# Three inner norms by split products with constant tiles and one root function, in a one-core decoder step

## The chip, the cores and the metric

The kernel runs on one core of one Trainium2 chip. Its time is that of one execution on the device, in microseconds (us). The core has five engines that work side by side, each through its own queue in order: TensorE (PE in the profile, its weight loads PEld), VectorE (DVE), ScalarE (ACT), GpSimd (POOL) and SyncE (SP), which here only issues transfers. GpSimd and ScalarE can issue transfers too. An instruction that has to wait for another engine holds up everything behind it in its own queue.

## The reference

One inference step of one decoder layer for 256 prompt positions and 8 x 4 sample positions, 288 columns in all, at a model width of 2048:

```python
h = rmsnorm(x, norm1_g)
proj = h @ w_in + b_in                      # 2048 -> 3 x 1024: a, gate, z
u = a * sigmoid(gate)
c = silu(layernorm(depthwise_causal_conv(u, 31 taps), ln_g, ln_b))
p = (multiscale_pool(z) grouped @ pool_w) * pool_scale
x = x + concat(c, p) @ w_out                # 2048 -> 2048
h2 = rmsnorm(x, norm2_g)
x = x + square(relu(h2 @ w_ff1)) @ w_ff2    # 2048 -> 8192 -> 2048
y = rmsnorm(x, norm_f)
```

All inputs are float32. So there are four norms: the first before `w_in`, the layer norm of the conv channels in the middle, the one before the MLP, and the last. The first three are called the inner norms here.

## The kernel before

Activations are kept transposed, channels on the 128 partitions and the 288 columns on the free axis. All large products are made in fp32r from split operands: a float32 tile is cast to fp32r (its high part), the rest is subtracted (its low part), and a product is the sum of three: high by high, low weight by high input, high weight by low input. Weights arrive in blocks of 128x1024 (`wr`), ScalarE casts them (`whi`, L274), and the low part (`wlo`) is made by VectorE (way "V", L279), by GpSimd in two halves (way "G", L282), or by a ScalarE copy of -high (L276) and a transfer issued by GpSimd that adds the block once more from memory (way "D", L277). `WAYS` says which block goes which way; the seven "D" blocks lie in the input projection.

The weights pass in a fixed order: input projection (conv pairs c0 to c7 and pool groups p0 to p3 by `SEQUENCE`), `w_out` of the pool half, `w_out` of the conv half, the MLP. TensorE's order is that of the code: `mm` (L302) chains its products by `issue_after` while `chain` is set, and `between` of `gemm` puts a norm's products at a given place among them. The other engines' order is set by a scheduler, from priorities (`later(by)` lowers them, a negative value raises them) and an estimate of readiness; buffers of the pools decide when a block can follow.

The norms are never applied to an input before its product. The product of the unnormed input is made, and the result is multiplied by a row of 1/root, copied over all partitions:

- first norm: `squares` adds up the squares of x on VectorE and ScalarE, `rsqrt_sums` (L238) sums over partitions with a ones column on TensorE (float32, 96 columns by 1, three times), makes the root and three refinement steps on 96x3 numbers on VectorE, and `spread` (L259) turns that into a row `rb` on 128 partitions with three products by the identity and a ScalarE copy. `conv_pair` multiplies gate and value by `rb`, makes u, and GpSimd makes the sample positions' tap products (`prd`, L464), VectorE the prompt's taps (L461).
- middle norm: `ln_mean` makes the mean with two float32 products by `ones`, `ln_sums` subtracts it, squares and sums, then `rsqrt_sums` and, 24 products later, `spread`. `mixc` (L592 to L598) multiplies, applies silu and splits: the tiles `mx`, inputs of the second half of `w_out`.
- third norm (`second_rows`, L638): split sums times the constant tile `means`, root by ScalarE, `inverse_root` (L231) on full rows of 288.
- last norm: sums of 96x3, `inverse_root`, spreading, multiplication and the way out.

At the start nine float32 products of `ones` keep TensorE busy (L214) while the first weights and inputs come in. `first_split` (L359) prepares the first blocks: ScalarE casts, VectorE scales the first input tile (L367), and subtracts (L373, L376).

## Time and profile before

| | |
|---|---|
| runs, us | 1084.41, 1084.62, 1085.51; median 1084.62 |
| profiled execution, us | 1084.57 |
| its span, us | 1082.8 |
| TensorE busy in the span | 99% |
| VectorE, ScalarE, GpSimd | 59%, 44%, 16% |
| GpSimd busy between 40.5 and 55.3 us | 14.74 of 14.80 us |
| memory traffic, GB/s: first three 40ths of the span, mean | 325, 281, 273; 176 |
| transfers issued by GpSimd | 7, of 512 KB, 5.8 to 9.8 us from issue to landing |

The page's share of busy time is an average over stages. Rows of a timeline read: start (us from the span's start), duration in us, engine, line, operation, written tile <- read tiles, shapes, count of instructions merged into the row, and in brackets how long the engine was idle before and what ended that. Buffer numbers are left out. A float32 product shows as two rows' worth of passes, so nine warm products are x18. In a row of a stretch of time (`40.50:55.30 ...`) stand its length, then busy time and count of PE, PEld, DVE, ACT and POOL, then the granted clock (filled with 1.00 where the trace has no record), the share of the transfer engines and GB/s.

### The profile page before, as it was taken

To read this page: it belongs to the slowest core of one execution; us is meant where nothing else is said; L and a number is where in the kernel's file an instruction comes from. 1 tells how busy PE (TensorE), PEld (TensorE's weight loads), DVE (VectorE), ACT (ScalarE), POOL (GpSimd) and SP (SyncE) were. 2 spreads that over 40 slices of the span, in tenths; PEclk is the share of its full clock that TensorE was granted. 3 is DMA by queue.
4 is the path that set the end of the run, shared out by engine and by line. 5 is a ranking of instruction groups with operands and counts; after the bars stand their busy time and mean duration, and the time that the engine had idled before them with its cause. 6 is when DMAs were issued, how large, how long until landed. Compare 5 with 4: busy or idle time off the path is not lost.

```text
span 1082.8 us, 19572 instructions
## 1 busy us (share of the span) xinstructions
PE 1071.5 (99%) x8198; PEld 1069.9 (99%) x8198; DVE 635.4 (59%) x818; ACT 479.0 (44%) x585; POOL 173.6 (16%) x180
## 2 busy tenths in 40 slices
PE   9999999999999999999999999999999999999996
PEld 9999999999999999999999999999999999999996
DVE  8899999678655544445544444545544445554553
ACT  8654445475544433334443333444433334444441
POOL 0878979512000000000000000000000000000001
PEclk9999999999999999999999999999999999999998
DMA  9896468545555555555555555555555555555522
GB/s 325 281 273 185 137 196 239 176 152 177 173 164 170 172 166 169 174 164 169 171 168 168 175 165 169 174 167 167 174 165 168 174 169 165 173 166 168 173 78 88
DMA packets 58296, 190.71 MB, mean 176 GB/s; under 512 B 6240, under 2 KB 11232, under 8 KB 58208
## 3 DMA queue, kind: packets, MB, share of 16 engines
q1 hardware_dynamic: 56336, 184.35, 53.9%
q0 software_dynamic: 1008, 3.67, 1.9%
q8 instruction: 64, 1.05, 0.4%
q10 hardware_dynamic: 864, 1.44, 0.4%
q14 instruction: 24, 0.20, 0.1%
HBM read 185.16 MB, written 4.28 MB: 175 GB/s over the span
## 4 chain that ended last, share of the span: by engine, by line
PE 77%; issue 20%; ACT 1%; DVE 0%; DMA 0%; POOL 0%; POOLq 0%
PE ac L305 77%; PE pp L305 1%; DMA wr<-in_w 0%; ACT whi L274 0%; POOL xT L720 0%; ACT n L595 0%; DVE wlo L279 0%; PE pt L305 0%; PE pmean L305 0%; POOLq L770 0%; DVE xT L695 0%; DVE n L592 0%; ACT whi L364 0%; ACT mx L597 0%; DVE hx L367 0%
## 5 line engine op out<-in xcount | busy, mean ns | idle before, releaser
L274 ACT CAST whi<-wr 128x1024 fp32r<-128x1024 f32 (+1 forms) x332 | 348.0, 1049 | 551.4 <-PE ac L305 533.5
L279 DVE TENSOR_TENSOR wlo<-wr,whi 128x1024 fp32r<-128x1024 f32 x288 | 353.1, 1226 | 348.5 <-ACT whi L274 348.5
L305 PE MATMUL ac<-ax,whi 128*128 128x288 f32 x2048 | 351.0, 292 | 0.0
L305 PE MATMUL ac<-fx,whi 128*128 128x288 f32 x2048 | 350.2, 292 | 0.0
L305 PEld LDWEIGHTS ac<-ax,whi 128*128 128x128 f32 x2048 | 296.0, 187 | 0.0
L305 PEld LDWEIGHTS ac<-fx,whi 128*128 128x128 f32 x2048 | 295.6, 187 | 0.0
L305 PE MATMUL ac<-ax,wlo 128*128 128x288 f32 x1024 | 217.4, 292 | 0.0
L305 PE MATMUL ac<-fx,wlo 128*128 128x288 f32 x1024 | 216.4, 292 | 0.0
L305 PEld LDWEIGHTS ac<-ax,wlo 128*128 128x128 f32 x1024 | 162.6, 187 | 0.0
L305 PEld LDWEIGHTS ac<-fx,wlo 128*128 128x128 f32 x1024 | 162.3, 187 | 0.0
L305 PE MATMUL ac<-hx,whi 128*128 128x288 f32 x768 | 131.8, 295 | 1.2 <-DVE hx L367 1.2
L720 POOL TENSOR_TENSOR xT<-xT,rf 128x288 f32<-128x288 f32 x4 | 3.1, 795 | 800.1 <-ACT rf L724 800.1
L305 PEld LDWEIGHTS ac<-hx,whi 128*128 128x128 f32 x768 | 112.1, 190 | 1.4 <-ACT hx L369 1.4
L282 POOL TENSOR_TENSOR wlo<-wr,whi 128x512 fp32r<-128x512 f32 x74 | 100.3, 1410 | 35.3 <-ACT whi L274 34.3
L461 DVE SCALAR_TENSOR_TENSOR pc<-u_all,vec,pc 128x256 f32<-128x256 f32 x232 | 99.5, 483 | 1.9 <-ACT pc L458 0.7
L305 PE MATMUL ac<-hx,wlo 128*128 128x288 f32 x384 | 80.1, 294 | 0.0
L305 PEld LDWEIGHTS ac<-hx,wlo 128*128 128x128 f32 x384 | 61.1, 190 | 0.0
L305 PE MATMUL ac<-dx,whi 128*128 128x288 f32 x256 | 46.0, 296 | 0.0
L305 PE MATMUL ac<-mx,whi 128*128 128x288 f32 x256 | 45.1, 294 | 0.1
L664 DVE SCALAR_TENSOR_TENSOR t<-ac,r 128x576 f32<-128x576 f32 x32 | 24.2, 758 | 25.1 <-PE ac L305 25.1
L305 PEld LDWEIGHTS ac<-dx,whi 128*128 128x128 f32 x256 | 38.0, 188 | 0.2
L305 PEld LDWEIGHTS ac<-mx,whi 128*128 128x128 f32 x256 | 37.5, 188 | 0.6 <-ACT mx L597 0.4
(133 smaller groups left out, 533.6 us busy)
## 6 DMA issues: line engine op xcount, KB each, us to landing
wr<-in_w SPq DMA_DIRECT2D x335, 512.0 KB, 3.8
wlo<-in_w POOLq DMA_DIRECT2D x7, 512.0 KB, 7.7
xT<-in_xT SPq DMA_DIRECT2D x8, 288.0 KB, 7.3
wr<-in_w SPq DMA_DIRECT2D x5, 256.0 KB, 3.6
out_u_out<-u_all SPq DMA_DIRECT2D x1, 1208.0 KB, 9.3
u_all<-in_hist_c SPq DMA_DIRECT2D x8, 136.0 KB, 6.2
out_z_out<-z_all SPq DMA_DIRECT2D x1, 668.0 KB, 9.9
z_all<-in_hist_p SPq DMA_DIRECT2D x4, 152.0 KB, 7.5
```

Source lines behind the costliest of these rows:

```text
L274: nc.scalar.copy(hi, raw)
L279: nc.vector.tensor_tensor(lo, raw, f32(hi), op=ALU.subtract)
L282: nc.gpsimd.tensor_tensor(lo[:, j : j + 2, :], raw[:, j : j + 2, :], f32(hi[:, j : j + 2, :]), op=ALU.subtract)
L305: last = nc.tensor.matmul(*args, **kw)
L461: nc.vector.scalar_tensor_tensor(out=dst, in0=up[:, w : w + SEQ], scalar=cwv[:, w : w + 1], in1=pc, op0=ALU.mult, op1=ALU.add)
L664: nc.vector.scalar_tensor_tensor(out=t, in0=bk[:, :, :T], scalar=0.0, in1=both(rows2[0]), op0=ALU.max, op1=ALU.mult)
L720: eng.tensor_tensor(xk, xk, r[:, None, :].to_broadcast([P, n, T]), op=ALU.mult)
```

## The change

- Warm products: 13 in place of 9. The first scaled input tile is issued ahead of VectorE's first subtractions. The table loaded at the start, before the middle norm and before the third is that of `Abs_reciprocal_sqrt` instead of `Sqrt`.
- `inverse_root` now makes the 1/root in one ScalarE function with epsilon as its bias, and three refinement steps on VectorE; the reciprocal is gone. `rsqrt_sums` and `spread` are gone.
- First norm: the summed squares are split (cast on ScalarE, subtraction on VectorE), two fp32r products by `means` give the mean on all partitions, and `inverse_root` works on full rows of 288. All of it stands at one place of TensorE's queue, inside the third pair's products.
- Middle norm: the two summands of the mean are split (one on GpSimd, one on VectorE), four fp32r products by a new constant tile `means_c`; the sums are split, two products, `inverse_root` on full rows, at one place 60 products before the first one of `mx`.
- VectorE's additions and subtractions of the middle norm are written as `scalar_tensor_tensor`, the form of the taps. Several pieces get a raised priority.

```diff
-    for j in range(9):
+    for j in range(13):
         nc.tensor.matmul(warm[:, 0, 0:P], ones, ones, start=True, stop=True)
...
+    means_c = const.tile([P, P], F32R, name="means_c")
+    nc.gpsimd.tensor_scalar(means_c, ones, 1.0, None, op0=ALU.mult)
...
-    def inverse_root(mean, root, y, out):
+    def inverse_root(mean, y, t, out, after=None):
-        nc.vector.reciprocal(y, root)
-        nc.vector.scalar_tensor_tensor(out=root, in0=mean, scalar=EPS, in1=y, op0=ALU.add, op1=ALU.mult)
...
+        nc.scalar.activation(y, mean, AF.Abs_reciprocal_sqrt, bias=eps[: y.shape[0], :])
         if after is not None:
+            load_table(after, y[:, 0:1])
+        nc.vector.scalar_tensor_tensor(out=t, in0=mean, scalar=EPS, in1=y, op0=ALU.add, op1=ALU.mult)
+        nc.vector.scalar_tensor_tensor(out=t, in0=t, scalar=-0.5, in1=y, op0=ALU.mult, op1=ALU.mult)
+        nc.vector.scalar_tensor_tensor(out=out, in0=t, scalar=1.5, in1=y, op0=ALU.add, op1=ALU.mult)
...
             if k == 0:
-                nc.vector.tensor_scalar(hx[k][0], xT[:, k, :], v("norm1_g", k), None, op0=ALU.mult)
+                first = nc.vector.tensor_scalar(hx[k][0], xT[:, k, :], v("norm1_g", k), None, op0=ALU.mult)
...
         for b in blocks:
-            nc.vector.tensor_tensor(lo[:, b], raw[:, b], f32(hi[:, b]), op=ALU.subtract)
+            with tc.issue_after(first.ins) if k0 == 0 else nullcontext():
+                nc.vector.tensor_tensor(lo[:, b], raw[:, b], f32(hi[:, b]), op=ALU.subtract)
...
-        return [tot[0][:, 0, :]]
+        hs1 = actp.tile([P, 4, T], F32R, name="hs1", tag="p", bufs=4)
+        split_sums = [hs1[:, k, :] for k in range(2)]
+        nc.scalar.copy(split_sums[1], tot[0][:, 0, :])
+        nc.vector.scalar_tensor_tensor(out=split_sums[0], in0=tot[0][:, 0, :], scalar=1.0, in1=f32(split_sums[1]), op0=ALU.mult, op1=ALU.subtract)
+        return split_sums
...
     def first_sums():
-        diag.append(rsqrt_sums(squares(), 1.0 / D, AF.Sigmoid))
-        return diag[0][2]
-
-    def first_rows():
-        pr, last = spread(diag[0])
-        nc.scalar.copy(rb, pr)
+        with later(-LATER):
+            bk = ms("pt")
+            mean, root = bk[:, 0, :T], bk[:, 1, :T]
+            for j, part in enumerate(squares()[::-1]):
+                last = mm(mean, means, part, start=j == 0, stop=j == 1)
+            inverse_root(mean, tmp("y"), root, rb, after=AF.Sigmoid)
         return last
...
-    third = conv_products(2, between={2: first_rows}, classes="01" * 9 + TURN)
+    third = conv_products(2, between={2: first_sums}, classes="01" * 9 + TURN)
...
     def ln_mean():
         norm["mean"] = ms("pmean")[:, 0, :T]
-        mm(norm["mean"], ones, sum_c[:, 0, :], start=True, stop=False)
-        return mm(norm["mean"], ones, cs[-1][:, 1, :], start=False, stop=True)
+        return products(norm["mean"], [hm[:, j, :] for j in (1, 0, 3, 2)])
...
+            hs = actp.tile([P, 4, T], F32R, name="hs", tag="act")
+            low_part(nc.vector, hs[:, 0, :], ssc[:, 0, :], hs[:, 1, :])
+            bk, rl = ms("pt"), row("rl")
+            last = products(bk[:, 0, :T], [hs[:, 1, :], hs[:, 0, :]])
+            norm["rows"] = bk[:, 1, :T]
+            inverse_root(bk[:, 0, :T], rl, norm["rows"], norm["rows"], after=AF.Silu)
         return last
...
-    BETWEEN = {5: {4: ln_mean}, 6: {6: ln_sums}, 7: {2: ln_rows}}
+    BETWEEN = {5: {4: ln_mean}, 6: {6: ln_sums}}
```

Where instructions stand now is shown for three places. GpSimd around its first two "D" transfers (`prd` are the tap products of the sample positions, `wlo` the low parts), before:

```order
L282 TENSOR_TENSOR wlo_608<-wr_603,whi_607 128x512 x2
L464 TENSOR_TENSOR prd_671<-u_all,vec 128x32x31
L464 TENSOR_TENSOR prd_712<-u_all,vec 128x32x31
L277 DMA wlo_613<-in_w 128x1024
L282 TENSOR_TENSOR wlo_622<-wr_617,whi_621 128x512 x2
L282 TENSOR_TENSOR wlo_627<-wr_619,whi_626 128x512 x2
L282 TENSOR_TENSOR wlo_862<-wr_857,whi_861 128x512 x2
L464 TENSOR_TENSOR prd_755<-u_all,vec 128x32x31
L277 DMA wlo_867<-in_w 128x1024
```

And after:

```order
L258 TENSOR_TENSOR wlo_610<-wr_605,whi_609 128x512 x2
L253 DMA wlo_615<-in_w 128x1024
L258 TENSOR_TENSOR wlo_624<-wr_619,whi_623 128x512 x2
L445 TENSOR_TENSOR prd_673<-u_all,vec 128x32x31
L445 TENSOR_TENSOR prd_714<-u_all,vec 128x32x31
L258 TENSOR_TENSOR wlo_629<-wr_621,whi_628 128x512 x2
L258 TENSOR_TENSOR wlo_864<-wr_859,whi_863 128x512 x2
L445 TENSOR_TENSOR prd_757<-u_all,vec 128x32x31
L253 DMA wlo_869<-in_w 128x1024
```

The first transfer and one pair of subtractions have moved ahead of the two tap products; the second transfer has the same work in front of it as before.

VectorE around the middle norm's sums (`q` the squares, `st` and `pt` the roots, `hs` the split sums), before:

```order
L571 TENSOR_TENSOR q_2690<-q_2690 128x288
L279 TENSOR_TENSOR wlo_2805<-wr_2798,whi_2804 128x1024
L249 TENSOR_SCALAR st_2709<-pt_2705 96x3
L253 RECIPROCAL st_2709<-st_2709 96x3
L254 TENSOR_TENSOR st_2709<-st_2709 96x3
L255 SCALAR_TENSOR_TENSOR st_2709<-st_2709 96x3
L256 SCALAR_TENSOR_TENSOR st_2709<-st_2709 96x3
```

And after:

```order
L569 SCALAR_TENSOR_TENSOR q_2699<-q_2699 128x288
L255 TENSOR_TENSOR wlo_2811<-wr_2804,whi_2810 128x1024
L540 SCALAR_TENSOR_TENSOR hs<-q_2699,hs 128x288
L238 SCALAR_TENSOR_TENSOR pt_2717<-pt_2717,rl_2718 128x288
L239 SCALAR_TENSOR_TENSOR pt_2717<-pt_2717,rl_2718 128x288
```

The low half of the sums stands behind the subtraction of a weight block that stood behind TensorE's sums before.

ScalarE from the middle norm's sums to the first normed channels (`n` the silu steps, `mx` their high parts), before:

```order
L274 CAST whi_2804<-wr_2798 128x1024
L250 ACTIVATE st_2709<-st_2709 96x3
L209 ACT_TABLE_LOAD
L209 ACTIVATE few<-st_2709 96x1
L274 CAST whi_2891<-wr_2887 128x1024
L595 ACTIVATE n_2809<-n_2809,vec 128x288 x2
L274 CAST whi_2895<-wr_2889 128x1024
L595 ACTIVATE n_2816<-n_2816,vec 128x288 x2
L597 CAST mx_2813<-n_2809 128x576
```

And after:

```order
L250 CAST whi_2810<-wr_2804 128x1024
L538 CAST hs<-q_2699 128x288
L235 ACTIVATE rl_2718<-pt_2717,cst 128x288
L209 ACT_TABLE_LOAD
L209 ACTIVATE few<-rl_2718,ones 128x1
L250 CAST whi_2897<-wr_2893 128x1024
L250 CAST whi_2901<-wr_2895 128x1024
L595 ACTIVATE n_2815<-n_2815,vec 128x288 x2
L595 ACTIVATE n_2822<-n_2822,vec 128x288 x2
L597 CAST mx_2819<-n_2815 128x576
```

The cast of the high half stands behind a cast of weights, and two casts of weights instead of one now stand ahead of the first silu steps.

More of the change, by code (lines that the diff above doesn't have):

```diff
@@ L572, in ln_sums @@
-        norm["sums"] = rsqrt_sums([ssc[:, 0, :]], 1.0 / DC, AF.Silu)
-        return norm["sums"][2]
-    def ln_rows():
-        norm["rows"], last = spread(norm["sums"])
+        with later(-LATER):
+            ssc = None
+            for c in cs:
+                nc.vector.tensor_tensor(c, c, norm["mean"][:, None, :].to_broadcast([P, 2, T]), op=ALU.subtract)
+                q = tmpp.tile([P, 2, T], F32, name=nm("q2"), tag="ag" if ssc is None else "ag2", bufs=2)
+                nc.scalar.activation(q, c, AF.Square)
+                if ssc is None:
+                    ssc = q
+                else:
+                    nc.vector.scalar_tensor_tensor(out=ssc, in0=ssc, scalar=1.0, in1=q, op0=ALU.mult, op1=ALU.add)
+            nc.vector.scalar_tensor_tensor(out=ssc[:, 0, :], in0=ssc[:, 0, :], scalar=1.0, in1=ssc[:, 1, :], op0=ALU.mult, op1=ALU.add)
+            hs = actp.tile([P, 4, T], F32R, name="hs", tag="act")
[4 more added lines that the diff above has]
+            inverse_root(bk[:, 0, :T], rl, norm["rows"], norm["rows"], after=AF.Silu)
@@ L647, in second_rows @@
         last = mm(mean, means, lo, start=False, stop=True)
-        nc.scalar.activation(root, mean, AF.Sqrt, bias=eps)
-        inverse_root(mean, root, r2, r2)
+        inverse_root(mean, r2, root, r2)
         rows2.append(r2)
```

75 lines of the change are left out of this document (27 added, 48 removed).

## The prediction

> **What bounds the kernel now.** First the engine table and the waits of TensorE, then the chain that ended last, then the timeline at three places. The table and the list of TensorE's waits:
>
> ```profile
> PE 1071.5 (99%) x8198; PEld 1069.9 (99%) x8198; DVE 635.4 (59%) x818; ACT 479.0 (44%) x585; POOL 173.6 (16%) x180
> ...
> PE ac L305 <- DVE hx L367: 1.2, 1, 1.2
> PE ends L712 <- DVE cst L236: 0.2, 1, 0.2
> ```
>
> TensorE is busy 99% of the span. Between warm-up and end it waits once for long, 1.2 us at the very start, and 0.2 us in the last norm. So a step counts only if it takes work off TensorE's own queue, makes its products run faster, or makes TensorE wait where it did not. Durations below are of the profiled execution (1084.57 us: span 1082.8 and 1.8 around it), which agrees with the median of the runs, 1084.62.
>
> Its products, and what the norms add among them, in the chain that ended last:
>
> ```profile
> 32.63 0.43 PE pt L305 x6
> ...
> 35.81 0.84 PE pt L305 x6
> 36.65 73.54 PE ac L305 x564
> ...
> 201.31 0.97 PE pmean L305 x4
> ```
>
> A product of 128x288 costs 73.54/564 = 0.130 us of the stream. The first norm puts 0.43 (sums) and 0.84 (spreading) into it, the middle one 0.97 for its mean and again 0.43 + 0.84.
>
> **Removed products.** First norm: 1.27 becomes two products, 0.26: -1.0 us. Middle norm: 0.97 + 1.27 = 2.24 becomes four and two products, 0.78: -1.46 us. Both would be gains if nothing waited in their place.
>
> **The start.** The warm-up, VectorE's first steps and the first products:
>
> ```profile
> 1.04 4.21 PE L214 MATMUL warm<-ones 128*128 128x128 f32 x18 [1.04 <-DVE cst L229]
> 5.28 0.69 DVE L373 TENSOR_TENSOR wlo<-wr,whi 128x512 fp32r<-128x512 f32 x1 [2.88 <-ACT whi L364]
> 5.89 0.36 DVE L367 TENSOR_SCALAR hx<-xT,vec 128x288 fp32r<-128x288 f32 x1
> 6.40 1.30 PE L305 MATMUL ac<-hx,whi 128*128 128x288 f32 x4 [1.15 <-DVE hx L367]
> ...
> 8.45 2.12 PE L305 MATMUL ac<-hx,whi 128*128 128x288 f32 x8
> ...
> 10.37 0.79 PE L305 MATMUL ac<-hx,wlo 128*128 128x288 f32 x4
> 11.00 1.76 PE L305 MATMUL ac<-hx,whi 128*128 128x288 f32 x12
> ```
>
> The nine warm products (18 passes) end 1.15 us before the first real one, and the 16 real products from 6.40 to 10.37 take 3.97/16 = 0.248 us each, twice the later pace: the clock came up only near 10.4. Thirteen are 26 passes, 26 x 4.21/18 = 6.1 us, until about 7.1: the gap closes. If the clock is up by then, 16 products save 16 x (0.248 - 0.130) = 1.9 us, less up to 0.5 us by which slow warm passes hold the first product back. If it comes up no sooner than before, only those 0.5 us are lost. The scaled input is issued ahead of the subtraction, which frees at most the 0.3 us of that subtraction left in the way, and only if the warm passes are done. I take -1.4 (bounds -2.2 and +0.5), near the saving, since 6.1 us without a gap and the products behind them make over 7 us of dense work, where 4.2 with a gap did not do. [...]
>
> So TensorE reaches the second half of the input projection about 1.0 + 1.4 = 2.4 us earlier, and the question is what is ready for it.
>
> **What is late next: GpSimd's transfers.** Seven low halves of weights are made by a transfer that GpSimd issues after a copy on ScalarE (way "D", L276 and L277). GpSimd's rows up to the second of them, its share of the stretch (busy 14.74), the landing of that transfer and of all seven, and the product that reads it:
>
> ```profile
> 32.94 2.54 POOL L282 TENSOR_TENSOR wlo<-wr,whi 128x512 fp32r<-128x512 f32 x2
> ...
> 40.56 4.33 POOL L464 TENSOR_TENSOR prd<-u_all,vec 128x992 f32<-128x992 f32 x2 [0.94 <-DVE u_all L449]
> 44.83 1.06 POOL L277 DMA_DIRECT2D wlo<-in_w  x1
> ...
> 55.28 1.14 POOL L277 DMA_DIRECT2D wlo<-in_w  x1
> ...
> 40.50:55.30 14.80, 14.80 (x115) 14.80 (x115) 13.51 (x31) 9.04 (x12) 14.74 (x11) 1.00 0.74 210
> ...
> DMA to landing us min/median/max: 7.7/7.7/7.7
> ...
> DMA to landing us min/median/max: 5.8/7.7/9.8
> ...
> 63.39 0.42 PE L305 MATMUL ac<-hx,wlo 128*128 128x288 f32 x2
> ```
>
> GpSimd works without a pause from 40.56 to the issue at 55.28. That transfer lands at 55.28 + 7.7 = 63.0, and its first product stands at 63.39: 0.4 us to spare, in a kernel that is to arrive 2.4 us earlier. Does the transfer move too? Its ScalarE copy and the root of the first norm:
>
> ```profile
> 36.80 0.39 ACT L530 COPY rb<-pt 128x288 f32<-128x288 f32 x1
> 40.08 1.06 ACT L276 ACTIVATE wlo<-whi 128x1024 fp32r<-128x1024 f32 x1
> ...
> 285.40 0.48 ACT L648 ACTIVATE mean<-mean,cst 128x288 f32<-128x288 f32 x1
> ...
> 289.41 0.46 DVE L235 SCALAR_TENSOR_TENSOR mean<-mean,r 128x288 f32<-128x288 f32 x1
> ```
>
> In the new order ScalarE's root stands behind the same casts as the copy of the row did, so at about 36.8; now it is followed by three VectorE steps of full rows, 0.48 + 3 x 0.52 (0.46 and the hop to the next) = 2.0, and the row is ready near 38.9 instead of 37.2. What waits for it (the four multiplications, the gates, the tap products of GpSimd) comes 1.7 us later. GpSimd has been given other work there: the first transfer and two subtractions now go ahead of the tap products. The first transfer can be issued when its ScalarE copy is done: 36.8 + 0.48 + 1.28 (table) + 0.2 + 1.05 (cast) + 1.06 = 40.9. From there GpSimd has the same 14.7 us to the second: issue at 55.6, landing at 63.3 with the old 7.7, at 61.4 with the shortest latency of the seven. TensorE, due at 61.0, waits for it. Of the 2.4 us, 0.1 us is left by the one and 2.0 by the other. I keep 0.6: the latency is nearer to its median, a little less because the first transfer now lands earlier and out of its way. [...]
>
> **The middle norm.** ScalarE, VectorE and TensorE around its sums:
>
> ```profile
> 208.75 1.06 ACT L274 CAST whi<-wr 128x1024 fp32r<-128x1024 f32 x1 [1.61 <-issue]
> 208.94 0.46 DVE L571 TENSOR_TENSOR q<-q 128x288 f32<-128x288 f32 x1
> 209.84 1.23 DVE L279 TENSOR_TENSOR wlo<-wr,whi 128x1024 fp32r<-128x1024 f32 x1 [0.44 <-ACT whi L274]
> 210.11 0.59 PE L305 MATMUL pt<-ones,q 128*96 128x1 f32 x6
> ...
> 215.79 1.15 ACT L595 ACTIVATE n<-n,vec 128x288 f32<-128x288 f32 x2 [1.96 <-DVE n L592]
> 216.85 1.03 ACT L274 CAST whi<-wr 128x1024 fp32r<-128x1024 f32 x1
> 218.84 1.23 ACT L597 CAST mx<-n 128x576 fp32r<-128x576 f32 x2
> 219.55 0.30 PEld L305 LDWEIGHTS ac<-mx,whi 128*128 128x128 f32 x2 [0.35 <-ACT mx L597]
> ```
>
> Counted from the start of the mean (201.2), everything before the sums moves 0.45 us up with the shorter mean. The sums are then ready at 208.95, but have to be split: the high half stands behind a cast of weights on ScalarE (208.3 to 209.4) and ends at 209.8, the low half on VectorE stands behind that block's subtraction (to 210.6) and ends near 211.0. The two products have their place at 201.2 + 0.52 + 60 x 0.13 = 209.5: TensorE waits 1.3 us or so inside the norm. They end at 211.1, and 60 products lead to the first product of the normed channels, due at 219.0. For it ScalarE now has two casts of weights ahead of the first silu. The second takes a buffer that TensorE frees: the cast at 208.75 waited 1.61 us for such a release, and releases are 24 products (3.1 us) apart, so the one after next comes at 208.7 + 6.2 + the norm's own products, near 216. Cast 1.05, four silu steps at 0.58, one cast of 0.62: ready at 219.8 where before the product stood at 219.55 (its weight load 0.35 us behind, by its row). The 1.46 us of removed products are spent, and +0.3 us on top (bounds -0.7, if the second cast is released early, and +0.8).
>
> **Last norm and the rest.** The removed reciprocals, and the last input of the middle norm's mean:
>
> ```profile
> 285.91 1.96 DVE L233 RECIPROCAL r<-mean 128x288 f32<-128x288 f32 x1 [0.56 <-ACT mean L648]
> ...
> 1071.57 0.17 DVE L233 RECIPROCAL cst<-cst 96x3 f32<-96x3 f32 x1 [1.53 <-ACT cst L708]
> ...
> 195.80 0.48 DVE L461 SCALAR_TENSOR_TENSOR c<-u_all,vec,pc 128x256 f32<-128x256 f32 x1
> ```
>
> In the last norm TensorE waits 0.2 us in all, so -0.2 at most, and the reciprocal's 0.17 is that. The 1.96 us in the norm before the MLP are worth nothing: TensorE has no wait there, its products cover it. The table loads stay five. VectorE's steps in another form keep their durations (0.46 for 288 columns in either form here). The splits for the middle norm's mean cost nothing: its last input was ready at 195.80 + 0.48 = 196.3, the mean starts at 201.2, and a cast and a subtraction take 0.9; if these 4 us go, TensorE waits by the rest.
>
> **Sum.** -0.6 (start and first norm, what the transfer leaves) + 0.3 (middle norm) - 0.2 (last norm) = -0.5: 1084.57 - 0.5 = 1084.1 us. Its own range is -1.9 to +0.9, 1082.7 to 1085.5. A difference of under 0.2%, 2.2 us, is about what counts as no change here.
>
> **Rivals.** (1) Everything removed shows: the transfers land first, the norm's splits fit. -1.0 - 1.4 - 1.46 - 0.3 - 0.2 = -4.4, 1080.2 us. For it: the shortest landing, 5.8, nearly allows the start; against it: the splits stand behind two weight steps in two queues. Chance 0.1. [...] (2) Slower, by contention of GpSimd and VectorE:
>
> ```profile
> 34.27 1.22 DVE L255 SCALAR_TENSOR_TENSOR st<-st 96x3 f32<-96x3 f32 x1
> 35.52 0.16 DVE L256 SCALAR_TENSOR_TENSOR st<-st 96x3 f32<-96x3 f32 x1
> ```
>
> The first step of 96x3 took 1.22 us while GpSimd's subtraction of 32.94 ran, its like after it 0.16. The new low half of the first sums reads two SBUF tiles at that very place, and so do the subtractions in GpSimd's unbroken run. One hold of 1.1 us makes the row and GpSimd's run 1.1 us later, the transfer lands at 64.4, the product stands 1.0 behind its old place: 1.0 + 0.3 - 0.2 = +1.1, 1085.7. It decides from a landing at 65.5 on, two holds; with two and a half, 2.7 us, the transfer lands at 66.0: 2.6 + 0.3 - 0.2 = +2.7, 1087.3 us. Chance of that 0.1. (3) The warm products do nothing, the clock comes up as late as before: the start loses 0.5, the first norm's 1.0 is eaten at the transfer, 1084.6 us. Chance 0.1, inside no change. The forecast has 0.7.
>
> Faster 0.1 (rival 1), slower 0.1 (rival 2), same 0.8. The range for 8 in 10 reaches from 1082.2 to 1086.0.
>
> **What would show it.** Right: no gap before the first real products and these at 0.13 us each by 8 us; TensorE waiting 1 to 2.5 us near 61 to 64 for the transfer of wlo; a wait of about 1.3 us before the second sums product and one below 1 us at the first product of mx; no wait for a root in the last norm. Wrong: no wait at the transfer (then 1.7 us less), a split that comes out of a queue sooner than I read from the order, or a wait in the taps between 80 and 200 us, where I see none.

## The result

The changed kernel takes 1088.16 us (median of six runs, 1085.73 to 1090.81) beside 1084.51 for the kernel before: a ratio of 1.0032, 95% interval 1.0017 to 1.0047. It is 3.6 us slower. 1084.1 was forecast, with a range up to 1086.0. The runs scatter over 5 us, those of the kernel before over 1.6.

### The profile page after: what moved, and what is told of

Read it like the earlier page. It is cut to its first block, busy times and chain, and to the rows that moved or that the text cites. A ratio compares the mean times of both kernels' runs of the same rounds, so it can differ in the third digit from the quotient of the medians.

```text
span 1085.8 us, 19549 instructions
## 1 busy us (share of the span) xinstructions
PE 1070.1 (99%) x8186; PEld 1067.4 (98%) x8186; DVE 635.4 (59%) x815; ACT 479.3 (44%) x588; POOL 178.8 (16%) x182
## 3 DMA queue, kind: packets, MB, share of 16 engines
q8 instruction: 64, 1.05, 0.4%
## 4 chain that ended last, share of the span: by engine, by line
PE 71%; issue 21%; DVE 5%; ACT 1%; POOL 1%; DMA 1%; SPq 0%; POOLq 0%; DVEq 0%
PE ac L281 71%; DVE pc L442 2%; DVE wlo L255 1%; DMA wr<-in_w 1%; POOL s L473 0%; POOL wlo L258 0%; DVE dx L484 0%; PE pp L281 0%; DVE q L568 0%; ACT whi L250 0%; DVE d L478 0%; POOL xT L718 0%; DVE c L562 0%; ACT hx L345 0%; ACT n L595 0%
## 5 line engine op out<-in xcount | busy, mean ns | idle before, releaser
L255 DVE TENSOR_TENSOR wlo<-wr,whi 128x1024 fp32r<-128x1024 f32 x288 | 354.0, 1229 | 349.6 <-ACT whi L250 349.6
L258 POOL TENSOR_TENSOR wlo<-wr,whi 128x512 fp32r<-128x512 f32 x74 | 104.1, 1441 | 35.3 <-ACT whi L250 34.3
```

Source lines behind the costliest of these rows:

```text
L255: nc.vector.tensor_tensor(lo, raw, f32(hi), op=ALU.subtract)
L258: nc.gpsimd.tensor_tensor(lo[:, j : j + 2, :], raw[:, j : j + 2, :], f32(hi[:, j : j + 2, :]), op=ALU.subtract)
```

## The profile after

The profiled execution took 1087.62 us, span 1085.8. Its engine table and the waits of TensorE (us in total, times, longest):

```profile
PE 1070.1 (99%) x8186; PEld 1067.4 (98%) x8186; DVE 635.4 (59%) x815; ACT 479.3 (44%) x588; POOL 178.8 (16%) x182
...
PE ac L281 <- DVE wlo L255: 1.9, 1, 1.9
PE ac L281 <- ACT whi L347: 1.1, 1, 1.1
...
PE pt L281 <- DVE hs L540: 0.7, 1, 0.7
PE ac L281 <- ACT mx L597: 0.6, 1, 0.6
PE ac L281 <- ACT hx L345: 0.6, 1, 0.6
PE pp L281 <- DVE dx L484: 0.5, 1, 0.5
```

TensorE is busy 1.4 us less than before, and the span is 3.1 us longer. There are waits at the start (`hx`, `whi`), in the taps (`wlo` L255, `dx`), and in the middle norm (`hs`, `mx`); of the first two groups the page of before had one, of 1.2 us.

All kernels of this study pass the same 8112 large products (`ac` and `pp`) in the same order. So the start of the n-th of them, minus its start in the kernel before, tells where time is lost. From the two traces:

```
product      place                              start before   after - before, us
0            first real product                       6.40        -0.16
60           first pairs                             16.30        -0.67
180          end of the first pairs                  31.94        +0.55
220          behind the first norm                   38.63        -0.54
400          third and fourth pair                   62.09        -0.53
600          behind GpSimd's first transfers         88.14        +0.19
1120         taps, pool groups                      155.78        +0.19
1240         behind the last pool products          171.77        +3.31
1460         ahead of the middle norm               200.62        +3.29
1480         behind its mean                        204.24        +2.80
1540         behind its sums                        212.76        +3.79
1700         behind its rows                        235.42        +3.33
end          span                                  1082.75        +3.10
```

Of all the loss, 3.1 us lie between 156 and 172 us; the middle norm is level within 0.04. The chain that ended last passes VectorE there, where before it was TensorE's alone:

```profile
124.21 1.77 DVE d L478
...
130.68 2.51 DVE dx L484
...
166.59 1.70 DVE wlo L255
168.34 3.71 PE ac L281 x26
```

Two of these steps are far longer than their like. In the kernel before, `d` and `dx` of the same pool group (rows of VectorE's timeline):

```profile
127.57 0.69 DVE L497 SCALAR_TENSOR_TENSOR d<-s,z_all 128x512 f32<-128x512 f32 x1 [0.96 <-POOL s L496]
...
130.95 0.98 DVE L503 TENSOR_TENSOR dx<-d,dx 128x576 fp32r<-128x576 f32 x1
```

and in the changed kernel, first VectorE, then GpSimd:

```profile
124.21 1.77 DVE L478 SCALAR_TENSOR_TENSOR d<-s,z_all 128x512 f32<-128x512 f32 x1 [0.91 <-POOL s L477]
...
130.58 2.60 DVE L484 TENSOR_TENSOR dx<-d,dx 128x576 fp32r<-128x576 f32 x1
```

```profile
124.13 3.00 POOL L258 TENSOR_TENSOR wlo<-wr,whi 128x512 fp32r<-128x512 f32 x2
...
130.36 2.21 POOL L445 TENSOR_TENSOR prd<-u_all,vec 128x992 f32<-128x992 f32 x1 [1.25 <-DVE u_all L430]
```

`dx` started 0.22 us after GpSimd's tap products (`prd`) and ended 0.61 after their end: it was held for 1.86 us beyond its 0.74. `d` was held 1.09 in the same way by a subtraction that began 0.08 us ahead of it. Both read two inputs in SBUF. The taps (`pc`), one of whose inputs lies in PSUM, follow one another every 0.39 us beside GpSimd's next subtraction (three of them from 133.11 to 134.37 us). I call what happened to `d` and `dx` "held" below.

VectorE is behind for a second reason. The row `rb` is ready 1.05 us later (multiplications from 38.27 instead of 37.22), the first taps start at 43.67 instead of 41.71, and at 120 us it has done 125 taps where it had done 130: 2 us of work behind. The low part that it began at 135.73 us, after 150 taps, begins at 138.94 in the changed kernel, after 148: 3.2 us later with two taps less done, so another 2 us, about the two holds. In the kernel before there was little to give. The low part for which TensorE then waits longest and the product that needs it, before:

```profile
162.50 1.28 DVE L279 TENSOR_TENSOR wlo<-wr,whi 128x1024 fp32r<-128x1024 f32 x1
```

```profile
164.97 0.43 PE L305 MATMUL ac<-dx,wlo 128*128 128x288 f32 x2
```

and after:

```profile
166.51 1.77 DVE L255 TENSOR_TENSOR wlo<-wr,whi 128x1024 fp32r<-128x1024 f32 x1
```

```profile
168.34 0.54 PE L281 MATMUL ac<-dx,wlo 128*128 128x288 f32 x2 [1.88 <-DVE wlo L255]
```

Before, the one ended 1.2 us ahead of the other; now it ends 4.5 us later, and TensorE waits 1.9 us. At the `dx` that TensorE also waits for now (0.5 us, near 160 us), the slack was 0.5 us. A slack does not show among the waits.

## Experiments

Each kernel was profiled once and timed in 5 to 11 runs beside the kernel before. The table has the median, the ratio with its interval (taken over all runs, so it can differ from that of the medians), and from the profiled execution the gain (-) or loss (+) by stage, as differences of the ledger above (to 32 us; 32 to 88, with the first norm and the first transfers; 88 to 172, all of it from 156 on; 201 to 235, the middle norm), and the longest `dx<-d,dx` of VectorE:

```
kernel                      us        ratio [95%]            start  to 88  taps  middle  longest dx
changed kernel            1088.16  1.0032 [1.0017, 1.0047]   +0.55  -0.36  +3.12  +0.04    2.60
e1  sums early            1090.66  1.0045 [1.0033, 1.0057]   +0.03  +0.55   0.00  +5.73    1.82
e2  first norm old        1088.53  1.0032 [1.0020, 1.0045]   -0.33  +0.10  +0.02  +5.86    1.82
e3  first norm alone      1087.80  1.0029 [1.0019, 1.0040]   -0.68  +0.62  +3.11   0.00    2.59
e4  before, late row      1091.11  1.0060 [1.0048, 1.0072]   -0.03  +4.24  +1.92  +0.02    2.61
e5  e1, mean on GpSimd    1085.30  1.0009 [1.0001, 1.0018]   -0.77  -0.29   0.00  +2.53    1.79
e6  e1, other form        1088.89  1.0035 [1.0022, 1.0048]   -0.57  -0.47  +0.01  +5.64    1.79
e7  e1, middle norm old   1084.32  1.0000 [0.9991, 1.0009]    0.00  +1.75   0.00  +0.03    1.83
e8  start alone           1084.62  1.0003 [0.9994, 1.0012]   -1.23  +0.78  +0.01  +0.01    1.79
e9  e5, old sums          1084.26  0.9994 [0.9985, 1.0003]   -1.06  +0.56   0.00  +0.39    1.81
e10 e9, V for transfer 1  1087.33  1.0026 [1.0017, 1.0035]   -0.21  -1.18  +2.26  +1.29    2.60
e11 changed, dx on GpSimd 1091.38  1.0059 [1.0046, 1.0072]   -0.38  -1.09  +0.90  +5.81    1.78
e12 e9, G for transfer 2  1084.34  0.9996 [0.9987, 1.0005]   -0.70  +0.58   0.00  +0.43    1.83
e13 changed, mean GpSimd  1087.63  1.0033 [1.0021, 1.0044]   -0.74  +3.33  +4.64  +0.45    2.59
e14 e11 and e13           1087.63  1.0025 [1.0015, 1.0035]   -0.38  +0.38  +0.93  +2.48    1.80
e15 e9, sums at third     1087.40  1.0030 [1.0018, 1.0041]   -0.63  -1.10  +1.91  +1.30    2.60
```

### Is it the late row? (e1 to e4)

e1, the changed kernel with the first norm's two products where the old sums stood:

```diff
-    chain.append(gemm(pair0 + pair1, hx, classes="01" * 18 + TURN, by_part=True))
-    third = conv_products(2, between={2: first_sums}, classes="01" * 9 + TURN)
+    chain.append(gemm(pair0 + pair1, hx, between={15: first_sums}, classes="01" * 18 + TURN, by_part=True))
+    third = conv_products(2, classes="01" * 9 + TURN)
```

> The changed kernel with one edit: the two sums products of the first norm stand at the end of the first two pairs' products, where the old norm had its sums, instead of 24 products into the third pair. Theory V (VectorE late): the changed kernel loses its 3.3 us between 156 and 170 us because the first norm's row is ready 1 us later and the gates 2 us later, so that VectorE, which is without a pause from 130 us on, has five taps (2 us) more behind it when TensorE asks for its low parts. With the sums 3 us earlier the row is ready at about 35.5 us, VectorE's queue has the order of the kernel before, TensorE has no wait between 150 and 175, and the time is 1087.9 - 3.3 = 1084.5 us or a little below. Rival P (the raised priorities and the middle norm's splits put other work ahead in that stretch): the waits stay, 1087.5 us. Rival S (scatter of GpSimd's transfers): 1086 to 1088, with waits that move from run to run.

e2, the changed kernel with `rsqrt_sums` and `spread` back for the first norm:

```diff
-            for j, part in enumerate(squares()[::-1]):
-                last = mm(mean, means, part, start=j == 0, stop=j == 1)
-            inverse_root(mean, tmp("y"), root, rb, after=AF.Sigmoid)
+        diag.append(rsqrt_sums(squares(), 1.0 / D, AF.Sigmoid))   # sums at {15}, spread at {2}, as before
```

> The changed kernel with the first norm in its old form and places (sums of 96x3 by the ones column, spreading by the identity); only its root is the new ScalarE function, and all else (start, middle, third and last norm) stays changed. Theory V: the row is early again, no wait between 150 and 175; TensorE keeps the old norm's 1.0 us and the half microsecond that the start loses: 1087.9 - 3.3 + 1.0 = 1085.6 us at most, 1084.8 if GpSimd's second transfer then finds its old slack. Rival P: 1087.9 + 0.5 = 1088.4 us, the waits stay.

e3, the kernel before with the new first norm alone:

```diff
-        diag.append(rsqrt_sums(squares(), 1.0 / D, AF.Sigmoid))
+            inverse_root_new(mean, tmp("y"), root, rb, after=AF.Sigmoid)   # split sums, two products, at {2} of the third pair
```

> The kernel before with the new first norm alone (split sums, two products 24 products into the third pair, root by one ScalarE function, three full-row steps); start, middle, third and last norm as before. Theory V: VectorE's order is that of the changed kernel, and the waits of 156 to 170 us are all there: 1084.5 - 1.0 (products) + 3.3 = 1086.8 us. Rival P: nothing but the removed products shows, 1083.5 to 1084.5 us.

e4, the kernel before with a later row:

```diff
         nc.scalar.copy(rb, pr)
+        for _ in range(4):
+            nc.vector.tensor_scalar(rb, rb, 1.0, None, op0=ALU.mult)
```

> The kernel before with four more VectorE steps on the row of the first norm (each times 1.0, 128x288), which make it 1.9 us later; nothing else. Theory V: TensorE's products are the same, but VectorE starts its taps 2 us later and is three taps behind in the order at 70 to 120 us; the slack before the low parts at 168 to 171 us was 0.05 to 0.5 us, so TensorE waits there 1.5 to 2 us: 1086.0 to 1086.5 us. Rival P or S: 1084.5 us, the 1.9 us lie off the path.

In the taps theory V holds four times: with the row early (e1, e2) the loss there is 0.00 and 0.02, with the new first norm alone it is all there (e3, 3.11), and a late row alone brings 1.92 (e4). The raised priorities and the middle norm have no part in it. Theory V is too simple all the same. In e4 TensorE was 4.2 us late by 88 us, more than the row, and VectorE should have had time to spare; but its `dx` took 2.61 us there, as in the changed kernel and in e3. e3's time is 1.0 us above what was expected: its trace loses 1.7 us between 50 and 88 us, where one product comes 0.8 us late by a transfer and many run a little slower.

The times of e1 and e2 were missed by 6.2 and 2.9 us; that e2 came near the 1088.4 of its rival P is an accident, since the waits of the taps are gone. A loss of 5.7 and 5.9 appeared in the middle norm, which in the changed kernel costs nothing. VectorE of e1, then GpSimd beside it:

```profile
197.36 8.73 DVE L540 SCALAR_TENSOR_TENSOR hm<-c,hm 128x288 fp32r<-128x288 f32 x1 [0.50 <-ACT hm L538]
206.02 0.74 DVE L586 TENSOR_TENSOR xT<-xT,ac 128x576 f32<-128x576 f32 x1
```

```profile
197.53 0.85 POOL L542 TENSOR_TENSOR hm<-sum_c,hm 128x288 fp32r<-128x288 f32 x1
198.29 7.49 POOL L258 TENSOR_TENSOR wlo<-wr,whi 128x512 fp32r<-128x512 f32 x6
```

A subtraction that in the changed kernel took 0.70 us lasted 8.73: it was held through seven instructions of GpSimd and ended 0.31 us after the last. In e2 it was 8.75. TensorE waited for it 3.9 us, and the start of `c<-c,pmean` and all behind it moved. And e4's late row delayed GpSimd too: TensorE waited 1.9 us at 63 us for a transfer (`wlo<-in_w`), the second one, as the prediction had feared for the change itself.

These waits cost more than their length. Right behind them TensorE's granted clock is at half for 3.4 us, in e1 (length of the stretch, busy time and count of PE, PEld, DVE, ACT and POOL, granted clock, share of the transfer engines, GB/s):

```profile
206.30:209.60 3.30, 3.30 (x15) 3.30 (x16) 3.30 (x6) 2.03 (x3) 0.00 (x0) 0.50 0.51 165
209.70:213.00 3.30, 3.30 (x27) 3.30 (x26) 2.14 (x4) 1.64 (x2) 0.00 (x0) 1.00 0.00 0
```

The products there start 0.24 us apart instead of 0.13, so such a stretch costs about 1.5 us. It is part of the loss in the middle norm of e1, e2, e5, e6, e11 and e14, and in e4 it follows the wait at 63 us (65.5 to 68.9 us), which is why e4's time lies 4.6 us above what was expected. The profiled execution of the changed kernel has no such stretch between the warm-up and the end.

### The hold at the mean (e5, e6) and the rest of the middle norm (e7)

e5 and e6 differ from e1 by one line each:

```diff
-    low_part(nc.vector, hm[:, 2, :], cs[-1][:, 1, :], hm[:, 3, :])
+    low_part(nc.gpsimd, hm[:, 2, :], cs[-1][:, 1, :], hm[:, 3, :])   # e5
```

```diff
+    nc.scalar.copy(hm[:, 3, :], cs[-1][:, 1, :])   # e6: the same step as tensor_tensor
+    nc.vector.tensor_tensor(hm[:, 2, :], cs[-1][:, 1, :], f32(hm[:, 3, :]), op=ALU.subtract)
```

> The kernel of the early sums, with the low part of the last channel block's split for the middle norm's mean made by GpSimd instead of VectorE. In the trace of the early sums that VectorE step (c minus its high part, two inputs in SBUF) lasted 8.73 us, from 197.36 to 206.09, where its like takes 0.46 to 0.69, and it ended 0.3 us after GpSimd's unbroken run of subtractions; TensorE waited 3.9 us for it. Theory H (VectorE's step is kept out as long as GpSimd runs without a pause): on GpSimd the step takes its 0.8 us in the queue, the mean starts at its place near 201.7 without a wait, and the 5.2 us that are lost there go: 1090.7 - 4.7 to 5.2 = 1085.5 to 1086.0 us. Rival L (the split is late for another reason: the last tap, ScalarE's cast): the wait stays, 1089 to 1090.7 us.

> The kernel of the early sums, with that same VectorE step written as a plain tensor_tensor subtraction instead of the taps' form (scalar_tensor_tensor). Theory H (two inputs in SBUF beside GpSimd, whatever the form): the step is held again for several us, 1089.5 to 1091 us. Rival F (only the new form is held): the step takes 0.5 to 1.3 us, TensorE does not wait at the mean, 1085.5 to 1086 us.

The rows of that step, in e5 and in e6 (ns: shortest, median, longest):

```profile
L542 POOL TENSOR_TENSOR hm<-c,hm x1: 798/798/798, 199.2 to 199.2; 128x288 fp32r<-128x288 f32 x1
```

```profile
L547 DVE TENSOR_TENSOR hm<-c,hm x1: 8728/8728/8728, 195.7 to 195.7; 128x288 fp32r<-128x288 f32 x1
```

On GpSimd the hold is gone, the mean comes without a wait and gains 0.5 us, and the ratio falls from 1.0045 to 1.0009, by 3.9 us. In the other form the hold is the same to 0.01 us: the form of the instruction made no difference to it. An unbroken run of GpSimd is not enough for a long hold, though. In the changed kernel the same step began inside four subtractions of GpSimd that follow without a gap (197.14 to 202.45 us), and was let in after one of them:

```profile
L540 DVE SCALAR_TENSOR_TENSOR hm<-c,hm x1: 699/699/699, 200.6 to 200.6; 128x288 fp32r<-128x288 f32 x1
```

What is left in e5's middle norm is +2.5 us, in the sums: 2.5 us of waits and 1.5 at half the clock (211.9 to 215.3 us), less the 1.46 of removed products. VectorE's first addition of squares is held there too (2.16 us; 1.15 in the changed kernel), and what follows it comes late:

```profile
203.45 2.16 DVE L568 SCALAR_TENSOR_TENSOR q<-q,q 128x576 f32<-128x576 f32 x1
```

```profile
PE pt L281 <- ACT hs L538: 1.2, 1, 1.2
...
PE pt L281 <- DVE hs L540: 0.6, 1, 0.6
PE ac L281 <- ACT mx L597: 0.6, 1, 0.6
```

e7 puts the old middle norm (unsplit mean, sums of 96x3, spreading at `7: {2: ln_rows}`) into e1, so that the start, the first and the last norm stay:

```diff
-        return products(norm["mean"], [hm[:, j, :] for j in (1, 0, 3, 2)])
+        mm(norm["mean"], ones, sum_c[:, 0, :], start=True, stop=False)
+        return mm(norm["mean"], ones, cs[-1][:, 1, :], start=False, stop=True)
...
-    BETWEEN = {5: {4: ln_mean}, 6: {6: ln_sums}}
+    BETWEEN = {5: {4: ln_mean}, 6: {6: ln_sums}, 7: {2: ln_rows}}
```

> The kernel of the early sums, with the middle norm in its old form and places (mean by float32 products of the unsplit sums, sums of 96x3, spreading) but for the new root function. This leaves the start, the first norm at the old place and the last norm. Theory: all of the loss between 195 and 225 us (5.7 us in the trace of the early sums) is the new middle norm's, so 1084.8 + 0.6 (start, first norm, seen by 110 us) - 0.3 (last norm) = 1085.1 us, with no wait from 110 us to the end. If the start's half microsecond is an accident of that execution, 1084.3 us. Rival: another wait takes its place in the middle norm, 1087 us or more.

1084.32, a ratio of 1.0000: no wait in the taps and next to none in the middle norm, as expected. The profiled execution, 1086.16 us, is one of the slowest of its 11 runs; what holds it back is a wait for GpSimd's first transfer, near 51 us:

```profile
PE ac L308 <- DMA wlo<-in_w: 1.7, 1, 1.7
```

### The start alone (e8)

```diff
-    for j in range(9):
+    for j in range(13):
...
+            with tc.issue_after(first.ins) if k0 == 0 else nullcontext():
```

> The kernel before with the start alone changed (13 warm products, the first scaled input ahead of VectorE's subtractions). By the prediction's step the gain is 1.4 us when GpSimd's second transfer lands in time, 1083.4 us, and 0.6 with a wait there, 1084.2. By the three traces with 13 warm products (the clock is up by 5.5 us, but TensorE then waits 0.8 us between 17 and 19 us for an input tile and a low part, and is within 0.3 to 0.6 us of the old time at 32 us) it is nothing: 1084.5 to 1085.3 us, without a wait of 1 us at 61 to 64.

No difference, as expected from the traces: 1.0003 (0.9994 to 1.0012). The trace was 2.1 us ahead at 16 us, 1.2 at 32 and 0.45 at 88. The start cannot be read from one execution, though. With the nine old warm products, the warm-up of e3 and of e4:

```profile
1.04 3.63 PE L214 MATMUL warm<-ones 128*128 128x128 f32 x18 [1.04 <-DVE cst L229]
6.40 0.76 PE L314 MATMUL ac<-hx,whi 128*128 128x288 f32 x4 [1.72 <-DVE hx L376]
```

```profile
1.04 3.70 PE L214 MATMUL warm<-ones 128*128 128x128 f32 x18 [1.04 <-DVE cst L229]
6.62 0.76 PE L305 MATMUL ac<-hx,whi 128*128 128x288 f32 x4 [1.88 <-DVE hx L367]
```

These 18 passes took 4.21 us before; here the clock came up inside them, near 4 us, with nothing changed ahead of it. In e3 the first real products ran at full pace after a pause of 1.7 us; in e4, after one of 1.9, the clock was halved again from 7.5 to 10.9 us. When the clock comes up differs by execution: at 3.9, 4.1 and 10.6 us in the three traces with nine products (e3, e4, before), at 4.1 to 7.1 us in the 14 with thirteen.

### Towards a faster version (e9, e12), and the hold by order alone (e10, e15)

e9 is e5 with `ln_sums` and `ln_rows` in the old form. e12 and e10 change one letter of `WAYS` in it:

```diff
-"c3": "GDGG", "c4": "GDGD"
+"c3": "GVGG", "c4": "GDGD"   # e10: the first transfer becomes a subtraction on VectorE
+"c3": "GDGG", "c4": "GGGD"   # e12: the second becomes subtractions on GpSimd
```

e15 moves the first norm's products in e9 by eight products:

```diff
-    chain.append(gemm(pair0 + pair1, hx, between={15: first_sums}, classes="01" * 18 + TURN, by_part=True))
+    third = conv_products(2, between={0: first_sums}, classes="01" * 9 + TURN)
```

> The kernel with the early sums and the mean's split on GpSimd, with the second half of the middle norm (sums of 96x3, spreading) in its old form and place. Theory: the mean keeps the 0.5 us that it saved there (1.58 ahead of the kernel before at 204 us, 1.08 at 201), and the 3.0 us that the split sums lose (TensorE waits for the high and then the low half, and for the first normed channels) are gone: the trace ends 1.6 + 0.3 us below the span of before, 1082.6 us, when the first two transfers of GpSimd land in time; 1084 when one is 1.5 us late. Median between, 1083.3. Rival: the loss at the sums is not the new form's, 1085.3 us as with the mean's split alone.

> The same with the first of GpSimd's transfers replaced by a subtraction on VectorE (1.2 us of VectorE at about 48 us). It takes away the transfer that TensorE waited 2 us for in the trace with the old middle norm (near 51 us), so runs with that wait go: 1082.3 us with less scatter. Rival H2: the extra VectorE step shifts its order so that the second pool group's steps d and dx come four taps sooner, as in the changed kernel and unlike the old order; if they are then held beside GpSimd between 120 and 133 us (3.7 to 4.0 us of hold in the changed kernel, in the first norm alone and with the late row, 0.9 in the others), TensorE waits 1 to 3 us between 156 and 170 although the row is early: 1084 to 1086 us.

> As e9, with the second of GpSimd's transfers (issued near 55 us) replaced by GpSimd's own subtractions, 1.5 us more of GpSimd and no landing time. If TensorE's waits for transfers come from that one, 1082.6 us; if from the first, as in the trace with the old middle norm, no change against e9; if GpSimd's later transfers are pushed back by the 1.5 us and become late, 1 us slower than e9.

> The kernel of e9 with the first norm's two products 8 products later, at the head of the third pair, where their second input no longer comes 0.8 us after TensorE. If TensorE's own queue decides: 1084.3 - 0.8 = 1083.4 us. Theory H2: in VectorE's order the second pool group's d and dx come six taps sooner than in e9 (after 132 and 137 taps instead of 138 and 143), as in the changed kernel and in e10; there the steps are held for 3.9 to 4.0 us beside GpSimd between 120 and 150 us, and TensorE waits 2 to 3 us between 156 and 170: 1084.3 - 0.8 + 2.0 to 2.8 = 1085.5 to 1086.3 us.

e9 misses its 1083.3 by 1 us: in its trace the mean saves 0.45, but the old sums are asked for sooner than VectorE has them (0.9 us from product to product) and give it back. 0.9994 with an interval that holds 1: level with the kernel before. e12 is level with e9; neither trace has a wait for a transfer, so it says nothing about the second one.

e10 and e15 are the test of the hold. In both the row is early (first multiplications at 36.4 us, 37.2 in the kernel before); what they share with the changed kernel is VectorE's order, which has `d` and `dx` of the second pool group four to six taps sooner. The longest `dx` in e9, e10 and e15:

```profile
L511 DVE TENSOR_TENSOR dx<-d,dx x4: 744/1210/1808, 105.9 to 164.4; 128x576 fp32r<-128x576 f32 x4
```

```profile
L511 DVE TENSOR_TENSOR dx<-d,dx x4: 749/1080/2598, 105.4 to 166.2; 128x576 fp32r<-128x576 f32 x4
```

```profile
L511 DVE TENSOR_TENSOR dx<-d,dx x4: 745/1265/2595, 104.7 to 165.5; 128x576 fp32r<-128x576 f32 x4
```

The hold came in both, and with it 2.26 and 1.91 us of waits between 156 and 172 that e9 does not have. Their times, 1087.3 and 1087.4, lie 1.1 to 1.3 us above the end of what was expected of the hold; another 0.9 us (against e9) is lost in the middle norm, where TensorE now waits for the sums by 1.0 us.

### The changed kernel without its holds (e11, e13, e14)

```diff
-        nc.vector.tensor_tensor(dl, d, f32(dh), op=ALU.subtract)
+        (nc.gpsimd if g == 2 else nc.vector).tensor_tensor(dl, d, f32(dh), op=ALU.subtract)   # e11, e14
...
-    low_part(nc.vector, hm[:, 2, :], cs[-1][:, 1, :], hm[:, 3, :])
+    low_part(nc.gpsimd, hm[:, 2, :], cs[-1][:, 1, :], hm[:, 3, :])   # e13, e14
```

> The changed kernel with the low part of the second pool group's dx made by GpSimd instead of VectorE; the row stays as late as there. In the changed kernel that VectorE step took 2.60 us (130.58 to 133.18, 0.74 unheld). Theory H2 (VectorE's lateness at 156 to 170 us is 2 us from the late row and 2.3 us from steps held beside GpSimd): VectorE gets 2.6 us back, the waits there shrink from 3.3 to 0.5 to 1.3 us: 1087.9 - 2.0 to 2.8 = 1085.1 to 1085.9 us in an execution whose mean is not held. Rival V (the late row alone): VectorE gets only 0.74 us back, the waits are 2.5 us: 1087.2 us. GpSimd's own work, 1.6 us more, may come too late for the products of that group, which would show as a wait for dx near 145.

> The changed kernel, with the last channel block's low part for the middle norm's mean made by GpSimd instead of VectorE; nothing else, the row as late as there. In the profiled execution of the changed kernel that VectorE step took 0.69 us and nothing waited for it, but its runs reach from 1085.7 to 1090.8 us. Theory H: some of those runs contain a held step (up to 4 us), which goes; the waits of 156 to 170 us stay: 1087.0 to 1087.6 us, with the runs above 1088.5 gone. Rival: the scatter is of the transfers and the start, 1088.1 us and the same spread.

> The changed kernel with both steps on GpSimd: the second pool group's low part of dx (e11) and the mean's low part (e5). The row stays late, the start, the split sums and the last norm stay. Theory (late row 2 us, held steps 2.3 us, held mean): the trace of e11 was 0.6 us ahead of the kernel before at 200 us; without the hold at the mean it keeps that, gains 0.5 at the mean, loses 1.1 to 3 at the split sums and the first normed channels, and gains 0.3 at the end: 1084.5 - 0.6 - 0.5 + 2.0 - 0.3 = 1085.1 us (1084.3 to 1086.2). Rival: the waits move to another place, 1087 us or more.

e11 takes one VectorE step out, 0.74 us of work and 1.86 of hold, and the loss in the taps falls from 3.12 to 0.90 with the row as late as ever: two thirds of it hung on that step. The time rose all the same, to 1091.38, because TensorE now reached the mean early enough to run into the hold there (the step took 8.51 us; 3.9 us of wait, as in e1, and the half clock behind it). e14 removes both and keeps 0.93 in the taps, but pays 2.5 in the sums, as e5 did (the half clock included), and ends at 1087.63, not at 1085.1. So the changed kernel's losses replace one another: whichever comes first hides the others.

e13 keeps the loss in the taps and the scatter (1085.39 to 1091.94), so the scatter is not the hold at the mean; the rival was right. Its profiled execution, the slowest of its 11 runs (1091.94 us), shows where it may come from. TensorE, then a table of stretches (length, busy time of PE, PEld, DVE, ACT and POOL, granted clock, transfers):

```profile
61.05 0.68 PE L281 MATMUL ac<-hx,whi 128*128 128x288 f32 x4
63.84 0.53 PE L281 MATMUL ac<-hx,wlo 128*128 128x288 f32 x2 [2.11 <-DMA wlo<-in_w]
...
66.30 1.16 PE L281 MATMUL ac<-hx,whi 128*128 128x288 f32 x4
```

```profile
60.00:64.00 4.00, 1.89 (x15) 1.67 (x14) 4.00 (x12) 2.61 (x3) 4.00 (x3) 1.00 1.03 290
64.00:70.00 6.00, 6.00 (x35) 6.00 (x36) 6.00 (x14) 1.51 (x2) 1.07 (x2) 0.72 1.05 295
70.00:75.00 5.00, 5.00 (x40) 5.00 (x39) 1.56 (x4) 2.45 (x5) 2.93 (x3) 1.00 0.93 214
```

This is the wait for GpSimd's second transfer. Behind it the granted clock was at half from 65.2 to 68.6 us (0.72 is the mean of that row): together 4.1 us between products 400 and 480 of the ledger. In the taps TensorE's three waits are those of the changed kernel to 0.01 us. The longest was followed by another stretch at half the clock, 171.0 to 174.4 us, and that makes 4.64 of the changed kernel's 3.12. So equal waits can cost 1.5 us more in one execution than in another.

## Why the prediction was wrong

- **What is late next** is the step that failed. It found that the row comes 1.7 us later (measured 1.05, and 2.0 at the first taps), and followed that into GpSimd's queue alone. VectorE's queue of taps has the same row at its head and keeps the 2 us; the shifted order adds the held `d` and `dx`, and by 168 us a low part that had 1.2 us of slack comes 4.5 us later. The prediction named "a wait in the taps between 80 and 200 us, where I see none"; none was there because no wait is shown until slack is gone. 3.1 us in all: 0.9 are left when `dx` alone is taken off VectorE (e11, e14), and the shifted order alone, with an early row, costs 1.9 to 2.3 (e15, e10).
- **Contention** stood among the rivals with the right mechanism at another place: 1.1 us for one hold at the first sums. In the profiled execution that step was free (0.46 us); in eight of the 13 traces that have it, it took 1.53 to 1.55, as priced. The holds that cost time came at `d` (1.09) and `dx` (1.86), because the late row moved them in VectorE's order beside GpSimd's runs, and a third, of 8 us, waited at the mean in four other kernels. That the rival's 1087.3 us lies near the measured time is luck: it was to come by a late transfer.
- **The transfer**: no gap in the profiled execution (0.2 us lost at 62 to 64), since TensorE was 0.5 us ahead there and not 2.4. The mechanism is real: e7 lost 1.9 us near 51, and e13, where TensorE was 1.8 us ahead, had 2.4 us from one product to the next near 63 (e4, with its late row, 2.2). In e13 it cost 4.1 us with the half clock behind it.
- **The start**, -1.4, was mis-sized. That a stretch of dense work brings the clock up was the author's estimate, and no run shows it: with the nine old products it came up at 3.9 and 4.1 us as well (e3, e4). In the profiled execution it came up at 4.1 us, inside the warm products, so that these ended at 5.6 us and the gap did not close (0.6 us). The products ran at 0.13 by 8 us; but TensorE then waits for what ScalarE and VectorE bring (1.1 us at 8.6, 0.9 in all between 17 and 20), and at 32 us the profiled execution is 0.55 behind. Alone, it is worth nothing that can be measured (e8).
- **Removed products**: the first norm's 1.0 is right (+0.55 to -0.54 over it). In the middle norm, waits of 1.3 and below 1 were forecast at the second sums product and at the first `mx`; the second product came 1.07 us after the first, and the product of `mx` 0.92 after the one ahead of it. Net +0.04 where +0.3 stood. That is in part luck: in e5 and e14, where TensorE comes 2.4 to 4.4 us sooner and the first addition of squares is held longer, the same norm costs 2.5 us, 1.5 of them by the half clock, and 5.6 to 5.9 with the hold at the mean (e1, e2, e6, e11).
- **The mean's splits cost nothing**: so in the profiled execution (0.70 us, no wait). In e1, e2, e6 and e11 they cost 4.5 to 5.2 us, half clock included: their cover was taken as time, not as a queue beside GpSimd.
- **Last norm**, -0.2: right, -0.23 (3.33 behind at the last product, 3.10 at the end).

What is left open: how the six runs of the changed kernel divide between the waits and half clocks named, since only one of each kernel was profiled (the mean granted clock of its fastest run is 0.998 and of its slowest 0.995, which fits, but it also contains TensorE's idle end); and whether a version exists that beats the kernel before, which none of these did.

## What to carry to other kernels

When a change makes one row or tile later, follow it into every queue that has it at its head, up to the place with the least slack, and look up that slack from ends and starts; the list of waits shows nothing of it. Read the granted clock behind each wait: here half the clock added about 1.5 us behind some of them. Steps of VectorE with two inputs in SBUF had no fixed duration beside a busy GpSimd in these traces: the same new step on the way to TensorE took 0.70 us in the changed kernel and 8.73 in e1, where TensorE waited 3.9 us for it, and a mere shift in the order took the longest `dx` from 1.81 us (e9) to 2.60 (e15). One profiled execution of the new kernel shows one outcome of several; undoing a loss may uncover the next.

## What the runs showed of the hardware

- A VectorE step with two SBUF inputs that took 0.70 us in the changed kernel lasted 8.73, 8.75, 8.73 and 8.51 us in e1, e2, e6 and e11, through six or seven whole instructions of GpSimd. The seven of e1 follow one another without a gap from 197.53 to 205.78 us, and the step ended 0.31 us after the last. `d` and `dx` (1.77 and 2.60 us), and the same step in the changed kernel, ended 0.3 to 0.6 us after the end of one instruction of GpSimd. Why the step was let in there and not in e1 stays open.
- TensorE's granted clock was at half for 3.4 us behind some of its waits: behind 3.9 us in e1, 1.9 in e4 (65.5 to 68.9 us), 1.2 and 0.6 close together in e5 (211.9 to 215.3), and in e13 behind 2.1 (65.2 to 68.6) and 1.9 (171.0 to 174.4). It stayed at full behind the 1.9 us of the changed kernel at 168 us, the same wait as the second one of e13. So the length of a wait did not settle it, and what did is not shown. The ends of products are modelled, so the waits are estimates from these traces.
- In some stretches the products ran at 0.133 us instead of 0.130 (20 products in 2.67 us instead of 2.60) until about 85 us: in the changed kernel from 64 us, in e9 from 50 us with no wait ahead of it. That took 0.5 us from the changed kernel and 0.9 from e9. Its cause stays open.
